# Sample scores of the far cache rows: from transposes and products on TensorE to row sums on VectorE

## The chip, the core and the metric

The kernel runs on one core of a Trainium2 chip. The metric is device time in microseconds from the start to the end of one execution. A core has a matrix engine (PE; its weight loads are listed apart as PEld), VectorE (DVE), ScalarE (ACT), GpSimd (POOL), and SyncE (SP), which in this kernel issues nearly all the DMA transfers. Every engine works through its own instructions in order.

## The reference

One decoder layer works on a prompt of 2048 positions and on a sample: 8 batch rows of 8 new positions each, which follow a cache of 2048 older keys and values per batch row.

```python
h = _rmsnorm(x, norm_g)
z = jnp.einsum('bsd,dc->bsc', h, w_in)          # u, va, ga, q, k, vb, gb, each 512 wide
...
def _dilated_branch_sample(q, k_all, v_all, dil, n_strides):
    idx = w_buf + jnp.arange(T)[:, None] - dil * jnp.arange(n_strides + 1)[None, :]
    kg = k_all[:, idx]
    vg = v_all[:, idx]
    s = jnp.einsum('bthe,btjhe->bthj', q, kg).astype(jnp.float32) * (E ** -0.5)
    p = jnp.exp(s - m)
    o = jnp.einsum('bthj,btjhe->bthe', p, vg.astype(jnp.float32)) / den[..., None]
```

The sample attends with (window, dilation) = (128, 1), (512, 4) and (2048, 16), 8 heads of 64. So for a cache row further back than 512, new position t needs it only if its distance is a multiple of 16: of the first 1536 cache rows, t sees those whose index is t modulo 16, 96 of them. The last 512 rows are seen by several positions under masks. The prompt attends to itself with the same three dilations; gates, norms and an output projection follow.

## The kernel before, in words

The work is done in three stages, all laid out by one Python function whose order a scheduler then turns into one list per engine.

Stage 1 projects q, k and v of the prompt, tile after tile of 128 positions. A projection is a chain of 24 matrix products on two-part float16 operands (`product`, L258 to L275; the instruction is on L265), each 128x128 weights against 512 columns. I call these the dense products. Stage 2 is the prompt's attention, with mixer A's products between. Stage 3 (class `Fin`) does gate products (`ps_p`), merges the branches, and multiplies by `w_out` (`ps_y`), again 24 dense products to a chain.

The sample attention runs between the dense products of stage 1 (batch rows 0 to 4) and of stage 3 (batch rows 5 to 7; `NB1 = 5`). A generator, `Sample.batches`, hands out one small step at a time. After each dense product `pull_sample` credits it 216 ns times a rate (0.9 and 0.8), and a step costs `STEP1` or `STEP3`, so the two constants set how thickly the steps lie among the dense products. The small products are float32.

For one batch row the cache is read in `NC = 5` chunks of 128 partitions x 2 rows x 512 (`kr`, 512 KB, a ring of 3 buffers, loaded two chunks ahead by SP, L490). Chunks 0 to 3 are rows 16p+2g and 16p+2g+1, so they hold residues 0 to 7 of all 2048 rows; chunk 4 has the other residues of the last 512. Each chunk takes:

- 8 transposes on PE into PSUM (`ps_k`, L595), and two copies by ACT to SBUF (`kt`, L598);
- 8 products with the batch row's queries (`ps_q`, L499; 12 in the last chunk, which adds the new keys), 16 columns each: two heads by 8 positions. Every row is scored against all 8 positions, and a mask that VectorE adds (L507) throws most of that away.

`attend` then takes the maximum over all rows (VectorE L516; PE `ps_x` L520), subtracts it (PE `ps_b` L527, VectorE L528), exponentiates (ACT L529), sums (VectorE L530, PE `ps_n` L535), and multiplies the cached values in chunks `vr` (`ps_o`, L548: 8 products of 16 columns a chunk, 44 in all, after one product with zeros, L539). The score tile `sm` has `NK = 11` columns of 64.

Of the kernel before, what the change touches and what calls it, by code (L numbers as in the profile page):

```python
# [83 lines left out]
STEP1 = 250.0  # L84
STEP3 = 333.0
NK = 11
# [26 lines left out]
def kernel_body(tc, a):  # L113
# [34 lines left out]
    vsd = dram.tile([64, W], F32, name="vsd")  # L148
    hd = dram.tile([S + 64, W], F32, name="hd")
# [178 lines left out]
    def row_scale(t, x):  # L328

        n = P if t < NT else 64  # L330
        sq = [ph1.tile([P, 4, P], F32, name="sq", tag="sq") for _ in range(2)]
        for s_, x_ in zip(sq, x):
            small["sq", t] = act.activation(s_[:, :, :n], x_, AF.Square).ins
        a_, b_ = (s_[:, :, :n] for s_ in sq)
        pool.tensor_tensor(a_, a_, b_, op=ALU.add)
        dve.tensor_add(b_[:, 0:2], a_[:, 0:2], a_[:, 2:4])
        dve.tensor_add(b_[:, 0], b_[:, 0], b_[:, 1])
        ps = psR.tile([P, W], F32, name="ps_r", tag="R")
        small["r", t] = pe.matmul(ps[:n, 0:1], b_[:, 0], ones[:, 0:1], start=True, stop=True).ins
# [12 lines left out]
        return rb  # L352
# [71 lines left out]
    def operand(pool_, i, load=False):  # L424

        o = ops[i] = pool_.tile([P, DB, 4, 2 * T] if i == 0 else [P, 4, P], F32, name=("qbd", "ktn")[i], bufs=1)
# [43 lines left out]
    class Sample:  # L470
# [5 lines left out]

        def __init__(self, sam, samk, pso, step):
            self.sam, self.samk, self.step = sam, samk, step
            self.mask = const(samk, "smask", [P, 10 + DB, T], a["c_smask"])
            self.ps = pso.tile([P, W], F32, name="ps_q", bufs=1)  # L480
            self.po = pso.tile([P, 4, 2 * T], F32, name="ps_o", bufs=1)
            self.raws = {"kr": {}, "vr": {}}

        def load(self, c, key, u):
# [5 lines left out]
            sp.dma_start(r.rearrange("p n c -> p (n c)"), cache_rows(c, *u))  # L490

        def scores(self, b, g, kts, sm):

            o = (g // 2 % 2) * 4 + (g % 2) * 2
            for i in range(2 if g < NC - 1 else 3):
                for j in range(4):
                    c = (o + i) * G + j * 2 * T
                    k = kts[j // 2][:, j % 2, i * P:(i + 1) * P] if i < 2 else ops[1][:, j]
                    ii = pe.matmul(self.ps[:, c:c + 2 * T], k, ops[0][:, b, j], start=True, stop=True)  # L499
                    yield  # L500
            done.append(ii.ins)
            if g in (0, 2):
                return
            o = (g // 2 % 2) * 4
            lo = 4 * (g // 2)
            for i, n, m in ((0, 4, lo),) if g < NC - 1 else ((0, 2, lo), (2, 1, 10 + b)):
                dve.tensor_tensor(sm[:, lo + i:lo + i + n].rearrange("p n (c t) -> p n c t", t=T),  # L507
                                  self.ps[:, (o + i) * G:(o + i + n) * G].rearrange("p (n c t) -> p n c t", n=n, t=T),
                                  self.mask[:, m:m + n, None, :].to_broadcast([P, n, 8, T]), op=ALU.add)

        def attend(self, b, sm):
# [27 lines left out]
            keep(pe.matmul(po.rearrange("p j c -> p (j c)"), self.raws["vr"][(b, 0)][:, 0, 0:P], zero,  # L539
                           start=True, stop=False), "v")  # L540
            for g in range(NC):
# [25 lines left out]
        def batches(self, bs, keys_done=None):  # L567
# [8 lines left out]
            chunks = [(b, g) for b in bs for g in range(NC)]  # L576
# [5 lines left out]
            for b, g in chunks + [(None, g) for g in range(NC)]:  # L582
                if b is not None:
                    if g == 0:
                        sms[b] = self.sam.tile([P, NK, G], F32, name="sm", tag="sm", bufs=3)
                    kr = self.raws["kr"].pop((b, g))
                    self.load(ck, "kr", next(nxt, None))
                kts = []
                for x in range(2):
                    if b is not None:  # L590
# [6 lines left out]
                        kt = self.samk.tile([P, 2, 2 * P], F32, name="kt", tag="ktt", bufs=4)  # L597
                        act.activation(kt, ps, AF.Copy)  # L598
                        kts.append(kt)
                    if x and late:  # L600
# [3 lines left out]
                        if u[1] == NC - 1:  # L604
# [5 lines left out]
                if b is not None:  # L610
# [44 lines left out]
    def direct(t, raws, behind_=()):  # L655
# [3 lines left out]
        for g in range(0 if xg else 2):  # L659
            x = samk.tile([P, 4, P], F32, name="xg", tag="ktt", bufs=4)  # L660
# [708 lines left out]
def _constants():  # L1369
# [30 lines left out]
    p, i = np.arange(P), np.arange(10)[:, None]  # L1400
    key = np.where(i < 8, 16 * p + i, PAST - 4 * P + 16 * (p // 4) + 2 * (p % 4) + i).ravel()
# [4 lines left out]
    m = np.where(n > 0, 8.0 * np.log(np.maximum(n, 1)), NEG).reshape(10 + DB, P, T).transpose(1, 0, 2)  # L1406
# [45 lines left out]
```

## Time and profile before

| | us |
|---|---|
| median of 3 runs | 1211.02 |
| lowest, highest | 1210.85, 1211.27 |
| the profiled execution's own time | 1207.28 |
| its span, first to last instruction | 1205.5 |
| PE busy | 1146.0 (95%) |
| VectorE busy | 786.8 (65%) |
| ScalarE busy | 619.8 (51%) |
| granted PE clock, mean | 0.973 |

The span is what the profile sees; 1.8 us lie around it, and the profiled execution is 3.7 us under the median. A product's row has a duration that overlaps the next one, so what a product costs PE is the time from its start to the next start. A float32 product with 16 columns leaves two rows (two passes), a transpose one.

### The profile page before, as it was taken

The page shows a single profiled execution, that of the slowest core. Times are in us where ns is not written, and L with a number is a line of the kernel's source. Part 1 is how long each engine was busy: PE and PEld are TensorE (multiplying, and loading weights), DVE is VectorE, ACT ScalarE, POOL GpSimd, SP SyncE. Part 2 cuts the span into 40 slices and gives each one's busy share as a digit, 9 for nine tenths or more (in the row PEclk, how much of TensorE's full clock was granted, in tenths as well). Part 3 has the DMA queues.
Part 4 walks back from the last instruction along what each step waited for, and adds up shares of the span by engine and source line. Part 5 has one row for each costly group of instructions (what it writes and reads, how often), then busy time and mean ns, then how long its engine had stood idle before and what let it go on. Part 6 is the DMA issues. An engine that isn't in the chain of part 4 may idle for free. (4 is left out here: it accounts for less than half of the span.)

```text
span 1205.5 us, 23117 instructions
## 1 busy us (share of the span) xinstructions
PE 1146.0 (95%) x8402; PEld 752.3 (62%) x8402; DVE 786.8 (65%) x2332; ACT 619.8 (51%) x1341; POOL 274.9 (23%) x296
## 2 busy tenths in 40 slices
PE   7799999999999889999999999899989999999997
PEld 2347787877767346665766676566636667676543
DVE  7864445444442677877887887878955565665874
ACT  5564434343442746666776777867843332322332
POOL 4432122112110033243334334432300000000110
PEclk9899999999997999999999999999989999999999
DMA  8687676767572997879979978997699868576753
GB/s 272 203 299 221 186 222 198 241 194 214 172 232 81 246 228 170 142 137 228 180 145 194 222 132 180 194 177 126 155 322 335 236 202 235 162 189 184 208 137 96
DMA packets 299026, 237.98 MB, mean 197 GB/s; under 512 B 189920, under 2 KB 240096, under 8 KB 298912
## 3 DMA queue, kind: packets, MB, share of 16 engines
q1 hardware_dynamic: 272848, 210.58, 70.3%
q10 hardware_dynamic: 26064, 25.92, 7.4%
q8 instruction: 66, 1.08, 0.4%
q14 instruction: 48, 0.39, 0.1%
HBM read 128.38 MB, written 63.24 MB: 159 GB/s over the span
## 5 line engine op out<-in xcount | busy, mean ns | idle before, releaser
L265 PEld LDWEIGHTS <-xh 128*128 128x128 f16 x2712 | 288.7, 113 | 218.4 <-issue 30.2
L945 DVE CUSTOM_DVE_ANT_0 sm<-ps_s,mk,qsi 128x256 f32<-128x256 f32 (+1 forms) x384 | 145.1, 420 | 59.0 <-PE ps_s L940 44.0
L953 ACT ACTIVATE sm<-sm,st 128x256 f32<-128x256 f32 (+1 forms) x384 | 145.6, 450 | 57.6 <-DVE st L948 52.2
L265 PE MATMUL ps_y<-wh_o,cT 128*128 128x512 f16 x528 | 169.1, 380 | 0.0
L975 POOL TENSOR_TENSOR p<-sm,p 128x256 f16<-128x256 f32 (+1 forms) x128 | 112.8, 887 | 228.5 <-ACT p L974 202.9
L153 POOL TENSOR_TENSOR sc<-sc,powers 128x1 f32<-128x1 f32 (+3 forms) x51 | 31.5, 618 | 410.6 <-DVE sc L1151 189.4
L499 PEld LDWEIGHTS ps_q<-qbd,kt 128*128 128x128 f32 x640 | 107.9, 189 | 24.2 <-DVE sm L507 1.9
L548 PEld LDWEIGHTS ps_o<-sm,vr 128*128 128x128 f32 x640 | 109.2, 201 | 22.0 <-issue 1.1
L265 PEld LDWEIGHTS <-cT 128*128 128x128 f16 x800 | 82.0, 114 | 55.4
L265 PE MATMUL ps_y<-wl_o,cT 128*128 128x512 f16 x272 | 103.4, 380 | 0.0
L991 PE MATMUL ps_o<-vt,pT 128*128 128x65 f16 x600 | 78.9, 194 | 16.4 <-DMA pT<-p 16.2
L548 PE MATMUL ps_o<-sm,vr 128*128 128x16 f32 x640 | 93.5, 239 | 0.0
L499 PE MATMUL ps_q<-qbd,kt 128*128 128x16 f32 x640 | 91.1, 224 | 1.4 <-DVE sm L507 1.4
L265 PE MATMUL ps_p<-wh_v,xh 128*128 128x512 f16 x264 | 88.2, 382 | 2.1 <-DVE z L281 2.1
L265 PE MATMUL ps_p<-wh_va,xh 128*128 128x512 f16 x264 | 85.0, 389 | 3.4 <-ACT vt L384 3.0
L265 PE MATMUL ps_p<-wh_k,xh 128*128 128x512 f16 x248 | 82.5, 385 | 5.7 <-DVE xh L254 4.1
L265 PE MATMUL ps_p<-wh_gb,xh 128*128 128x512 f16 x264 | 86.7, 385 | 1.0 <-DVE u L1080 1.0
L265 PE MATMUL ps_p<-wh_u,xh 128*128 128x512 f16 x264 | 83.9, 379 | 1.7 <-DVE z L281 1.7
L265 PE MATMUL ps_p<-wh_ga,xh 128*128 128x512 f16 x264 | 85.4, 385 | 0.0
L936 PE MATMUL ps_s<-k,q 128*128 128x256 f16 (+1 forms) x384 | 83.0, 257 | 0.0
L940 PE MATMUL ps_s<-k,q 128*128 128x256 f16 (+1 forms) x384 | 82.2, 255 | 0.0
L598 ACT ACTIVATE kt<-ps_k 128x512 f32<-128x512 f32 x80 | 46.8, 591 | 65.0 <-PE ps_k L595 64.6
(308 smaller groups left out, 2578.8 us busy)
## 6 DMA issues: line engine op xcount, KB each, us to landing
vr<-cache_v SPq DMA_DIRECT2D x40, 512.0 KB
kr<-cache_k SPq DMA_DIRECT2D x40, 512.0 KB
xh<-xd SPq DMA_DIRECT2D x32, 512.0 KB
raw<-w_in SPq DMA_DIRECT2D x52, 256.0 KB
brd<-ob ACTq DMA_DIRECT2D x48, 264.0 KB
bt<-brd SPq DMA_DIRECT2D x16, 792.0 KB
vt<-vd ACTq DMA_DIRECT2D x48, 258.0 KB
vd<-vs SPq DMA_DIRECT2D x32, 258.0 KB
```

Source lines behind the costliest of these rows:

```text
L153: pool.tensor_tensor(out, src, powers[:out.shape[0], 0, 0:n], op=ALU.pow)
L265: ii = pe.matmul(out, l, r[:, k], start=(k == 0 and i == 0), stop=(k == 7 and i == len(ops) - 1))
L499: ii = pe.matmul(self.ps[:, c:c + 2 * T], k, ops[0][:, b, j], start=True, stop=True)
L548: ii = pe.matmul(po[:, j], v, sm[:, 2 * g + i, j * 2 * T:(j + 1) * 2 * T], start=False, stop=(g == NC - 1 and i == 2 and j == 3))
L598: act.activation(kt, ps, AF.Copy)
L936: ii = pe.matmul(out, q, kv[0], start=True, stop=False)
L940: keep(pe.matmul(out, q, kv[1], start=False, stop=True), "s")
L945: dve.tensor_tensor_reduce(sm[:, y].rearrange("p b k -> p (b k)")[:, 0:n], out, m, qsi[:, 3:4], -3e38, op0=ALU.add, op1=ALU.max, accum_out ...
L953: act.activation(sv, sv, AF.Exp, bias=self.st[:, 4 + u:5 + u], scale=1.0)
L975: (pool, dve)[x in DVELO].tensor_tensor(lo, sv, hi, op=ALU.subtract)
L991: keep(pe.matmul(po[:, u, 0:E + 1], hi, vv[:, vi, j, 0:E + 1], start=(b == 0), stop=False), "o")
```

## The change

Cache rows over 512 back are no longer scored on PE. The chunks become six, worked through in the order `KORD`: four far chunks of 96 partitions (`FAR`), where partition p holds rows 16p+2g and 16p+2g+1 of the first 1536, and two near chunks with the last 512 rows (four adjacent rows to a partition). The near chunks are transposed and scored as before. In a far chunk each of the two rows of a partition belongs to one new position t; its query row, kept in DRAM (`qsd`), is loaded broadcast to 96 partitions (`qb`, 192 KB), and VectorE multiplies the key row by it in place and sums each head's 64 elements (`far`). One column of `sm` then holds all far scores, with no mask, and the tile has 6 columns of 64 rather than 11. In `attend` a far value product has 96 rows of weights and 2 columns. `qb` shares the ring of `kt`, now 7 or 8 buffers rather than 4. `STEP1` and `STEP3` go up.

```diff
-STEP1 = 250.0
-STEP3 = 333.0
-NK = 11
+STEP1 = 310.0
+STEP3 = 480.0
+NK = 6
+FAR = 96
...
-        dg = ph1.tile([P, P], F32, name="dg", tag="dg")
+        dg = ph1.tile([P, P], F32, name="dg", tag="dg", bufs=1)
...
                 sample_operands(qk, i)
+                if i == 0:
+                    sp.dma_start(qsd, qk)
...
-            sp.dma_start(flat, opd[i])
+            sp.dma_start(flat, opd[i][:, b0 * 8 * T:] if i == 0 else opd[i])
...
-    NC = 5
+    NC = 6
+    FSTEP = 2
+    KORD = (0, 1, 4, 2, 3, 5)
...
         if g < 4:
-            return c[b].rearrange("(p r) c -> p (r c)", r=16)[:, 2 * g * W:(2 * g + 2) * W]
-        first = c[b, PAST - 4 * P + 8:PAST - 4 * P + 9, 0:1]
-        return bass.AP(tensor=c.tensor, offset=first.offset, ap=[[16 * W, 32], [2 * W, 4], [1, 2 * W]])
+            return c[b, 0:FAR * 16].rearrange("(p r) c -> p (r c)", r=16)[:, 2 * g * W:(2 * g + 2) * W]
+        return c[b, FAR * 16:].rearrange("(p r) c -> p (r c)", r=4)[:, 2 * (g - 4) * W:(2 * g - 6) * W]
...
+            self.kts = 7 if sam is samk else 8
...
-            sp.dma_start(r.rearrange("p n c -> p (n c)"), cache_rows(c, *u))
+            b, g = u
+            n = FAR if g < 4 else P
+            sp.dma_start(r[0:n].rearrange("p n c -> p (n c)"), cache_rows(c, b, g))
+            if key == "kr" and g < 4:
+                qs = self.qbs[u] = []
+                for t in (2 * g, 2 * g + 1):
+                    qs.append(self.samk.tile([P, W], F32, name="qb", tag="ktt", bufs=self.kts))
+                    sp.dma_start(qs[-1][0:FAR], qsd[b * T + t:b * T + t + 1].to_broadcast([FAR, W]))
...
+        def far(self, g, kr, qb, sm):
+
+            yield
+            for i in range(2):
+                k = kr[0:FAR, i]
+                ii = dve.tensor_tensor(k, k, qb[i][0:FAR], op=ALU.mult)
+                tc.add_manual_dep(ii.ins, tc_prod[0].name, AFTER, reason="not ahead of its place among the products")
+                o = sm[0:FAR, 0].rearrange("p (h t) -> p t h", t=T)[:, 2 * g + i]
+                dve.tensor_reduce(o, k.rearrange("p (h e) -> p h e", e=E), axis=AX.X, op=ALU.add)
+            yield
...
-                        v = (vr[:, i] if i < 2 else self.vn)[:, j * P:(j + 1) * P]
-                        ii = pe.matmul(po[:, j], v, sm[:, 2 * g + i, j * 2 * T:(j + 1) * 2 * T],
-                                       start=False, stop=(g == NC - 1 and i == 2 and j == 3))
+                        c = slice(j * 2 * T, (j + 1) * 2 * T)
+                        if g < 4:
+                            t = slice(2 * g + i, None, T)
+                            ii = pe.matmul(po[:, j, t], vr[0:FAR, i, j * P:(j + 1) * P], sm[0:FAR, 0, c][:, t],
+                                           start=False, stop=False)
...
                     if g == 0:
                         sms[b] = self.sam.tile([P, NK, G], F32, name="sm", tag="sm", bufs=3)
+                        dve.memset(sms[b][FAR:, 0], NEG)
...
                 for x in range(2):
-                    if b is not None:
+                    if far:
+                        next(fw)
+                        for _ in range(FSTEP):
+                            yield self.step
+                    elif b is not None:
...
-            x = samk.tile([P, 4, P], F32, name="xg", tag="ktt", bufs=4)
+            x = samk.tile([P, 4, P], F32, name="xg", tag="ktt", bufs=8)
```

PE, in the middle of stage 1, before: transposes of a key chunk (`ps_k`), each behind a dense product (`ps_p`).

```order
L595 MATMUL ps_k<-ident,kr 128x128
L265 LDWEIGHTS xh
L265 MATMUL ps_p<-wh_k,xh 128x512
L595 MATMUL ps_k<-ident,kr 128x128
L265 LDWEIGHTS xh
L265 MATMUL ps_p<-wh_k,xh 128x512
L595 MATMUL ps_k<-ident,kr 128x128
L265 LDWEIGHTS xh
L265 MATMUL ps_p<-wl_k,xh 128x512
L595 MATMUL ps_k<-ident,kr 128x128
```

And now, in the middle of stage 1, where values of a far chunk are multiplied (`ps_o`, 2 columns) and a far chunk of keys leaves no row on PE.

```order
L574 MATMUL ps_o<-sm,vr 128x2
L267 LDWEIGHTS xh
L267 MATMUL ps_p<-wh_k,xh 128x512
L574 MATMUL ps_o<-sm,vr 128x2
L267 LDWEIGHTS xh
L267 MATMUL ps_p<-wh_k,xh 128x512
L267 LDWEIGHTS xh
L267 MATMUL ps_p<-wl_k,xh 128x512
L267 LDWEIGHTS xh
L267 MATMUL ps_p<-wh_k,xh 128x512
```

Of 40 transposes and 44 score products a batch row, 16 and 20 are left; the value products become 52 (32 far, 20 near), and more dense products stand next to each other.

VectorE in stage 1, now: the products and sums of a far chunk (`kr`, `sm`) stand between the steps of the prompt's tiles (`vs`, `ss`, `dg`, `sq`) and of `attend` (`mx`).

```order
L545 TENSOR_REDUCE mx<-ps_x 64x1
L546 TENSOR_SCALAR mx<-ident,mx 64x64
L417 MEMSET vs 128x8
L418 SCALAR_TENSOR_TENSOR vs<-vt,qsc,vs 128x8x64
L529 TENSOR_TENSOR kr<-kr,qb 96x512 x2
L343 TENSOR_SCALAR ss<-ps_r 128x1
L532 TENSOR_REDUCE sm<-kr 96x8 x2
L338 TENSOR_TENSOR sq<-sq 128x256
L349 TENSOR_SCALAR dg<-ident,ss 128x128
L339 TENSOR_TENSOR sq<-sq 128x128
L552 TENSOR_TENSOR sm<-sm,ps_b 128x384
L554 TENSOR_REDUCE mx<-sm 128x64
```

Four such rows a far chunk, 16 a batch row, are new; a far chunk whose `kr` or `qb` has not landed holds up the rows behind it.

PE at the end of stage 1, before: the values of batch row 4 (`ps_o`) with few dense products left.

```order
L548 MATMUL ps_o<-sm,vr 128x16 x2
L535 MATMUL ps_n<-mx,ones 128x64
L548 MATMUL ps_o<-sm,vr 128x16 x22
...
L548 MATMUL ps_o<-sm,vr 128x16 x16
L548 MATMUL ps_o<-sm,vn 128x16
```

The same place now; where rows are left out stand 5 dense products before, and 6 now.

```order
L574 MATMUL ps_o<-sm,vr 128x2 x2
L559 MATMUL ps_n<-mx,ones 128x64
L574 MATMUL ps_o<-sm,vr 128x2 x22
...
L574 MATMUL ps_o<-sm,vr 128x2 x8
```

The first run keeps its length, and the second goes from 17 products to 8.

## Rows read from the trace of the kernel before

**Rows 1.** The page, part 1: busy time, share of the span and instructions by engine.

```profile
PE 1146.0 (95%) x8402; PEld 752.3 (62%) x8402; DVE 786.8 (65%) x2332; ACT 619.8 (51%) x1341; POOL 274.9 (23%) x296
```

**Rows 2.** Busy us by stretch: length, PE, PEld, DVE, ACT, POOL; clock, DMA share, GB/s.

```profile
40.00:50.00 10.00, 5.07 (x15) 1.89 (x14) 9.88 (x20) 5.87 (x12) 5.43 (x4) 0.91 0.32 98
...
103.00:350.00 247.00, 246.61 (x1766) 191.60 (x1767) 111.44 (x246) 102.79 (x165) 46.29 (x43) 1.00 0.68 208
...
365.00:383.00 18.00, 18.00 (x80) 14.98 (x80) 1.99 (x7) 2.02 (x4) 0.00 (x0) 0.53 0.29 86
...
890.00:905.00 15.00, 11.48 (x45) 5.54 (x43) 12.86 (x36) 8.41 (x16) 0.42 (x1) 0.77 1.06 387
905.00:1125.00 220.00, 220.00 (x1421) 151.55 (x1420) 131.26 (x265) 65.99 (x138) 12.92 (x21) 0.99 0.77 218
```

**Rows 3.** Timeline of PE in stage 1: start us, us, what, count.

```profile
304.07 0.29 PE L499 MATMUL ps_q<-qbd,kt 128*128 128x16 f32 x2
304.21 0.38 PE L265 MATMUL ps_p<-wh_k,xh 128*128 128x512 f16 x1
304.43 0.29 PE L499 MATMUL ps_q<-qbd,kt 128*128 128x16 f32 x2
...
304.78 0.60 PE L595 MATMUL ps_k<-ident,kr 128*128 128x128 f32 x4
305.22 0.29 PE L499 MATMUL ps_q<-qbd,kt 128*128 128x16 f32 x2
```

**Rows 4.** Timeline of PE in stage 1, at the value products.

```profile
340.88 0.29 PE L548 MATMUL ps_o<-sm,vr 128*128 128x16 f32 x2
341.02 0.38 PE L265 MATMUL ps_p<-wl_q,xh 128*128 128x512 f16 x1
```

**Rows 5.** Instructions of a line: count, duration ns least/median/most, first and last start.

```profile
L595 PE MATMUL ps_k<-ident,kr x320: 270/273/447, 76.0 to 1056.5; 128*128 128x128 f32 x160
L499 PE MATMUL ps_q<-qbd,kt x640: 176/262/283, 88.1 to 1075.1; 128*128 128x16 f32 x160
```

**Rows 6.** The same view, of VectorE's lines.

```profile
L1304 DVE TENSOR_TENSOR bt<-bt x16: 674/682/695, 897.4 to 1168.6; 128x512 f32<-128x512 f32 x16
...
L1299 DVE TENSOR_REDUCE mm<-dd x16: 158/180/183, 893.0 to 1164.4; 128x8 f32<-128x24 f32 x16
...
L521 DVE TENSOR_REDUCE mx<-ps_x x8: 272/282/283, 128.4 to 1090.7; 64x1 f32<-64x128 f32 x8
...
L516 DVE TENSOR_REDUCE mx<-sm x8: 1352/1362/1381, 121.6 to 1079.2; 128x64 f32<-128x704 f32 x8
```

**Rows 7.** Timeline around a product with 64 rows of weights (`ps_b`).

```profile
307.55 0.38 PE L265 MATMUL ps_p<-wh_v,xh 128*128 128x512 f16 x1
...
307.86 0.29 PEld L527 LDWEIGHTS ps_b<-mx,ones 64*128 64x128 f32 x2 [0.42 <-issue]
307.86 0.43 PE L527 MATMUL ps_b<-mx,ones 64*128 64x64 f32 x2
...
308.22 0.39 PE L265 MATMUL ps_p<-wh_v,xh 128*128 128x512 f16 x1
```

**Rows 8.** Timeline of PE at the end of stage 1.

```profile
362.65 6.80 PE L548 MATMUL ps_o<-sm,vr 128*128 128x16 f32 x44
369.29 0.59 PE L265 MATMUL ps_p<-wh_q,xh 128*128 128x512 f16 x1
```

**Rows 9.** Timeline of PE where the sample's part of stage 3 begins.

```profile
895.24 0.38 PE L265 MATMUL ps_p<-wh_gb,xh 128*128 128x512 f16 x1
899.13 1.94 PE L595 MATMUL ps_k<-ident,kr 128*128 128x128 f32 x8 [3.52 <-issue]
```

**Rows 10.** What SP's queue waited for: us in total, times, longest.

```profile
SPq L490 <- PE ps_o L548: 67.5, 25, 7.4
...
SPq L490 <- PE ps_k L595: 29.0, 19, 4.8
```

**Rows 11.** The page, part 2: DMA packets and bytes of the span.

```profile
DMA packets 299026, 237.98 MB, mean 197 GB/s; under 512 B 189920, under 2 KB 240096, under 8 KB 298912
```

More of the change, by code (lines that the diff above doesn't have):

```diff
@@ L148, in kernel_body @@
     vsd = dram.tile([64, W], F32, name="vsd")
+    qsd = dram.tile([64, W], F32, name="qsd")
     hd = dram.tile([S + 64, W], F32, name="hd")
@@ L424, in operand @@
     def operand(pool_, i, load=False):
-        o = ops[i] = pool_.tile([P, DB, 4, 2 * T] if i == 0 else [P, 4, P], F32, name=("qbd", "ktn")[i], bufs=1)
+        b0 = NB1 if load else 0
+        o = ops[i] = pool_.tile([P, DB - b0, 4, 2 * T] if i == 0 else [P, 4, P], F32, name=("qbd", "ktn")[i], bufs=1)
         flat = o.rearrange("p b j t -> p (b j t)") if i == 0 else o.rearrange("p j k -> p (j k)")
         if load:
-            sp.dma_start(flat, opd[i])
+            sp.dma_start(flat, opd[i][:, b0 * 8 * T:] if i == 0 else opd[i])
         else:
@@ L478, in __init__ @@
             self.sam, self.samk, self.step = sam, samk, step
-            self.mask = const(samk, "smask", [P, 10 + DB, T], a["c_smask"])
+            self.b0 = NB1 if sam is samk else 0
+            self.kts = 7 if sam is samk else 8
+            self.mask = const(samk, "smask", [P, 4 + DB, T], a["c_smask"])
             self.ps = pso.tile([P, W], F32, name="ps_q", bufs=1)
             self.po = pso.tile([P, 4, 2 * T], F32, name="ps_o", bufs=1)
-            self.raws = {"kr": {}, "vr": {}}
+            self.raws, self.qbs = {"kr": {}, "vr": {}}, {}
         def load(self, c, key, u):
@@ L489, in load @@
             r = self.raws[key][u] = pool_.tile([P, 2, W], F32, name=key, tag=key, bufs=3)
-            sp.dma_start(r.rearrange("p n c -> p (n c)"), cache_rows(c, *u))
+            b, g = u
[6 more added lines that the diff above has]
+                    sp.dma_start(qs[-1][0:FAR], qsd[b * T + t:b * T + t + 1].to_broadcast([FAR, W]))
         def scores(self, b, g, kts, sm):
-            o = (g // 2 % 2) * 4 + (g % 2) * 2
-            for i in range(2 if g < NC - 1 else 3):
+            x = g - 4
+            o = 4 * x
+            for i in range(2 + x):
                 for j in range(4):
@@ L498, in scores @@
                     k = kts[j // 2][:, j % 2, i * P:(i + 1) * P] if i < 2 else ops[1][:, j]
-                    ii = pe.matmul(self.ps[:, c:c + 2 * T], k, ops[0][:, b, j], start=True, stop=True)
+                    ii = pe.matmul(self.ps[:, c:c + 2 * T], k, ops[0][:, b - self.b0, j], start=True, stop=True)
                     yield
             done.append(ii.ins)
[L502 to L507, printed above, removed]
+            for i, n, m in ((0, 2, 2 * x), (2, 1, 4 + b))[:1 + x]:
+                dve.tensor_tensor(sm[:, 1 + 2 * x + i:1 + 2 * x + i + n].rearrange("p n (c t) -> p n c t", t=T),
                                   self.ps[:, (o + i) * G:(o + i + n) * G].rearrange("p (n c t) -> p n c t", n=n, t=T),
                                   self.mask[:, m:m + n, None, :].to_broadcast([P, n, 8, T]), op=ALU.add)
+        def far(self, g, kr, qb, sm):
[7 more added lines that the diff above has]
+            yield
         def attend(self, b, sm):
@@ L538, in attend @@
             zero = ops[1][:, 0, DB * T:]
-            keep(pe.matmul(po.rearrange("p j c -> p (j c)"), self.raws["vr"][(b, 0)][:, 0, 0:P], zero,
+            keep(pe.matmul(po.rearrange("p j c -> p (j c)"), self.raws["vr"][(b, 0)][0:FAR, 0, 0:P], zero[0:FAR],
                            start=True, stop=False), "v")
@@ L546, in attend @@
                     for j in range(4):
-                        v = (vr[:, i] if i < 2 else self.vn)[:, j * P:(j + 1) * P]
-                        ii = pe.matmul(po[:, j], v, sm[:, 2 * g + i, j * 2 * T:(j + 1) * 2 * T],
-                                       start=False, stop=(g == NC - 1 and i == 2 and j == 3))
+                        c = slice(j * 2 * T, (j + 1) * 2 * T)
[3 more added lines that the diff above has]
+                                           start=False, stop=False)
+                        else:
+                            v = (vr[:, i] if i < 2 else self.vn)[:, j * P:(j + 1) * P]
+                            ii = pe.matmul(po[:, j], v, sm[:, 2 * g - 7 + i, c],
+                                           start=False, stop=(g == NC - 1 and i == 2 and j == 3))
                         keep(ii, "v")
@@ L575, in batches @@
             bs = list(bs)
-            chunks = [(b, g) for b in bs for g in range(NC)]
+            chunks = [(b, g) for b in bs for g in KORD]
             nxt = iter(chunks)
@@ L588, in batches @@
                 kts = []
+                far = b is not None and g < 4
+                if far:
+                    fw = self.far(g, kr, self.qbs.pop((b, g)), sms[b])
                 for x in range(2):
-                    if b is not None:
+                    if far:
+                        next(fw)
+                        for _ in range(FSTEP):
+                            yield self.step
+                    elif b is not None:
                         ps = psT.tile([P, 2, 2 * P], F32, name="ps_k", tag="T")
@@ L596, in batches @@
                                 yield self.step
-                        kt = self.samk.tile([P, 2, 2 * P], F32, name="kt", tag="ktt", bufs=4)
+                        kt = self.samk.tile([P, 2, 2 * P], F32, name="kt", tag="ktt", bufs=self.kts)
                         act.activation(kt, ps, AF.Copy)
@@ L603, in batches @@
                             yield self.step
-                        if u[1] == NC - 1:
+                        if u[1] == KORD[-1]:
                             self.active.append(self.attend(u[0], sms.pop(u[0])))
@@ L609, in batches @@
                         yield from self.stage(work)
-                if b is not None:
+                if b is not None and not far:
                     late.append((b, g, kts, sms[b]))
@@ L1399, in _constants @@
     t = np.arange(T)
-    p, i = np.arange(P), np.arange(10)[:, None]
-    key = np.where(i < 8, 16 * p + i, PAST - 4 * P + 16 * (p // 4) + 2 * (p % 4) + i).ravel()
+    p, i = np.arange(P), np.arange(4)[:, None]
+    key = (PAST - 4 * P + 4 * p + i).ravel()
     own = np.where(p // T == np.arange(DB)[:, None], PAST + p % T, 10 * PAST).ravel()
@@ L1405, in _constants @@
     n = sum(((dist >= 0) & (dist <= P * d) & (dist % d == 0)).astype(int) for d in (1, 4, 16))
-    m = np.where(n > 0, 8.0 * np.log(np.maximum(n, 1)), NEG).reshape(10 + DB, P, T).transpose(1, 0, 2)
+    m = np.where(n > 0, 8.0 * np.log(np.maximum(n, 1)), NEG).reshape(4 + DB, P, T).transpose(1, 0, 2)
     out["c_smask"] = np.ascontiguousarray(m.astype(f))
```

## The prediction

> **What bounds the kernel now.** I read the page's busy times first, then the table by stretch, then PE's timeline, then what PE and SP wait for.
>
> By the busy times PE is at 95% and no other engine is over 65% [rows 1]. The table by stretch says where [rows 2]: in the two stretches that hold the sample attention, 103 to 350 us and 905 to 1125 us, PE is busy 246.61 of 247.00 us and 220.00 of 220.00. It never waits there. VectorE is busy 45% and 60% of these stretches, ScalarE 42% and 30%, the DMA engines 68% and 77%. So there the time is the sum of what PE has to do, and each product taken off its list shortens the kernel by its own start-to-start time, as long as nothing else becomes late.
>
> That time is read from the timeline [rows 3, 4]. A dense product takes 304.43 - 304.21 = 0.22 us. A score product takes 304.21 - 304.07 = 0.14 us, although it streams 16 columns. Four transposes take 305.22 - 304.78 = 0.44 us, 0.11 each. A value product takes 341.02 - 340.88 = 0.14 us.
>
> **The change part by part.**
>
> *PE's list.* Counts by batch row, 8 of them: transposes 40 to 16, scores 44 to 20, values 44 to 52. (The trace has 320 transposes [rows 5], which is 8 x 40.) So 192 transposes go, 192 x 0.11 = 21.1 us; 192 scores go, 192 x 0.14 = 26.9 us; 64 values come, 64 x 0.14 = 9.0 us. Net 39.0 us less, five eighths of it (24.4) in stage 1 and three eighths (14.6) in stage 3. All of it lies on the path, since PE does not wait in either place.
>
> The far value products are a new kind: 96 rows of weights, 2 columns. The trace has no such row. From below, their price is that of a transpose, 0.11 us: a product of 16 columns already costs 0.14, so its columns are not what it pays for. From above, there is a product with 64 rows of weights, `ps_b` [rows 7]. It starts 307.86 - 307.55 = 0.31 us after a dense product that needs 0.22, because its weights are not loaded until the product before is done (PEld stands idle 0.42 us and begins at 307.86 too), and the dense product behind it starts 0.36 us later, 0.45 in all. On 256 far value products that is 0.31 us more each, 79 us. I take 0.14, nearest in shape and type: the same matrix, three quarters of its rows.
>
> On this the Trainium skill has a rule, "TensorEngine Tiling (Array Packing)", sections Tiling Modes and Key Properties: a change of tiling mode drains the engine, and modes exist for 128, 64 and 32 rows. Rows 7 agree with the drain for 64 rows. By the page 96 rows fit no mode but the one of 128, there is no drain, and the sum stays at 39 us less; without that rule rows 7 could be stretched to 96 rows, and the sum would be 40 us more. No row here shows 96.
>
> *The clock at the end of stage 1.* Batch row 4's values come when the dense products run out: 22 in a row take 6.80 us [rows 8], and from 365 to 383 us the granted clock is 0.53, that is mostly 1.2 instead of 2.4 GHz, while PE is busy throughout [rows 2]. The 18 us lose about 8.5. The order now has the same first run, but the second has 8 products instead of 17. Nine at 6.80/22 = 0.31 us are 2.8 us less of the slow stretch. As they cost 0.17 more than the 0.14 already counted, and the dense products behind them get the full clock sooner, I take 2 us of gain (bounds 0 and 5).
>
> *VectorE.* A far chunk adds two products of 96x512 and two sums of 512 to 8, a batch row 8 of each. The product is bounded closely by a row of the same length, 0.68 us [rows 6]. For the sum the nearest rows are 24 elements to 8, 0.18 us, and 128 to 1, 0.28 us: 0.98 ns an element, so 0.18 + 488 x 0.98 ns = 0.66 us. From above, the sum over 704 strided elements takes 1.36, which for 512 would be 0.99. I take 0.66; the elements of a head lie next to each other. That is 8 x 1.34 = 10.7 us a batch row, up to 13.4. The two reductions over the score tile shrink from 704 elements to 384, 1.36 to about 0.74, 1.2 us less; net 9.5 us. Stage 1 gets 47 us more and stage 3 28. VectorE's load over the two stretches becomes about (111 + 40)/225 = 67% and (131 + 28)/206 = 77%. It stays under PE, which is what hides this. If that cover went, it would cost what VectorE is late by, at most these 75 us.
>
> *Waits that are new.* A far product waits on VectorE for three transfers (`kr` and two `qb`), and behind it stand the steps that the prompt's tiles need. Before, PE waited for `kr` itself, and it did so once, 3.52 us, at the beginning of stage 3 [rows 9], where the DMA engines are full (1.06) [rows 2]. SP now waits for VectorE before it may overwrite `kr`, where it waited 29.0 us in 19 times for the transposes [rows 10], and the loads and stores behind it on SP wait along; PE did not notice that in 905 to 1125. I bound what PE loses by 0 and by 3.52 us in every batch row, 28 us. I take 5, near the lower end, since a chunk is asked for two chunks ahead and PE has only these 3.52 us in the trace to show for all 40 key loads.
>
> *DMA.* Keys and values are the same bytes as before (4 x 384 + 2 x 512 KB against 5 x 512). The 64 broadcast loads add 64 x 96 x 2 KB = 12.6 MB to 238 [rows 11], 5%, in stretches with shares of 0.68 and 0.77 [rows 2]. Hidden. Eight of them and the store of `qsd` fall into the beginning, where the share drops to 0.32 between 40 and 50 us [rows 2]; I take nothing, with 2 us to either side.
>
> *The rest.* One `dg` buffer instead of two, the larger `xg` ring, the shorter operand load, a memset of 32 partitions a batch row, 48 fewer copies on ScalarE: each is off PE's list and hidden by PE's work; nothing.
>
> *Sum.* 1207.3 - 39.0 - 2 + 5 = 1171.3 for the profiled execution. The median of the runs stands 3.7 above that execution, so 1175.
>
> **The rivals.**
>
> *The far value products drain PE.* Place: the 256 products with 96 rows. Price 0.31 us each as from rows 7, 79 us, so 1175 + 79 = 1254. It decides from a price of 0.30 us a product on (0.14 + 40/256). For it: the only row with fewer than 128 rows of weights shows it. Against: 96 rows are more than half of the array, the far side of what that row has. This is the one that ends slower. The Trainium skill's page named above has no mode of 96 rows and speaks against it too.
>
> *VectorE or its transfers are late.* Waits as in rows 9 in every batch row: 23 us over the 5 that I took, 1198. For it: a chunk now lasts only a few dense products when `attend` has nothing to do, VectorE has up to 77% to do in order, and dense products of stage 3 need VectorE to empty their PSUM buffers. Against: rows 2, PE gapless with SP waiting a great deal.
>
> *More than the list.* The new waits do not come, and the beginning of stage 3 runs on: the 3.52 us gap of rows 9 goes, as PE's first rows there no longer need the first `kr`, and with it the low clock of 890 to 905 (0.77, some 3.4 us). 1175 - 5 - 3.5 - 3.4 = 1163.
>
> *It does not pay.* The steps are priced higher and spread wider, and what PE saves returns as waiting in order for products whose inputs are late. 1211. Against: the dense products need nothing from the sample.
>
> **How the numbers follow.** My forecast holds 0.62 (1166 to 1187), the list and more 0.13 (1157 to 1166), late VectorE 0.13 (1187 to 1205), the drain 0.09, no gain 0.03. The range leaves out the drain, no gain, and the tips of the others: 1160 to 1201. A measurement of this kernel can tell 0.2%, 2.4 us, from no change. Faster 0.62 + 0.13 + 0.13 = 0.88, same 0.02, slower 0.10 (the drain and a little of no gain).
>
> **What would show it.** PE's rows must be 192 transposes and 192 scores fewer, still gapless in the sample's stretches, with dense products 0.22 us apart. A far value product between two dense ones must take 0.14 us; 0.4 and an idle PEld before it is the drain. VectorE's new rows must take 0.68 and 0.66 us. The forecast is wrong if PE shows idle time before `ps_q`, `ps_x` or a dense product with VectorE or a DMA as the releaser, summing to more than 10 us, or if the granted clock drops in new places, where float32 products now run without dense ones between.

## The result, and the profile after

The changed kernel takes 1203.5 us in the median of 16 runs (1191.8 to 1214.5); the kernel before, beside it, 1211.6 (1208.4 to 1217.2). The ratio, which compares means, is 0.991, 95% interval 0.988 to 0.993. So the kernel is faster by 8 us in the medians and 11 by the ratio, where 36 were forecast, and its time is above the forecast's range (1160 to 1201). Two of the 16 runs, the slowest, are left out of the ratio and of the means below. The profiled execution took 1203.4 us, with a span of 1201.6.

The page's busy times, to be read against [rows 1]:

```profile
PE 1125.5 (94%) x7954; PEld 703.1 (59%) x7954; DVE 841.9 (70%) x2460; ACT 592.2 (49%) x1293; POOL 279.1 (23%) x296
```

The table by stretch of the changed kernel, same columns as [rows 2]:

```profile
103.00:350.00 247.00, 236.87 (x1516) 165.43 (x1515) 142.11 (x314) 88.40 (x141) 48.81 (x43) 0.96 0.81 235
365.00:383.00 18.00, 18.00 (x89) 14.16 (x89) 1.60 (x5) 1.41 (x2) 0.00 (x0) 0.62 0.32 104
890.00:905.00 15.00, 9.15 (x32) 3.89 (x32) 13.78 (x28) 5.67 (x12) 0.64 (x1) 0.77 1.05 244
905.00:1125.00 220.00, 212.67 (x1207) 127.20 (x1208) 153.79 (x320) 57.62 (x128) 16.13 (x23) 0.97 0.94 244
```

This is the result in four lines. PE, gapless before, now stands idle 247 - 236.87 = 10.1 us in the first long stretch and 7.3 in the last, and the granted clock is 0.96 and 0.97 where it was 1.00 and 0.99. The transfers take 0.81 and 0.94 of the DMA engines' time instead of 0.68 and 0.77. Over the whole span PE is idle 1201.6 - 1125.5 = 76.1 us, where it was 1205.5 - 1146.0 = 59.5.

What PE waited for in 40 to 368 us, in total, times and longest; first the two largest of before, then the changed kernel:

```profile
PE ps_p L265 <- DVE xh L254: 4.1, 1, 4.1
PE ps_p L265 <- DVE z L281: 2.1, 1, 2.1
```

```profile
PE ps_p L267 <- ACT qk L374: 5.0, 3, 3.3
PE ps_k L633 <- DMA kr<-cache_k: 4.6, 1, 4.6
PE ps_p L267 <- DVE xh L256: 3.9, 1, 3.9
PE ps_b L551 <- DVE mx L546: 2.2, 1, 2.2
PE ps_k L633 <- ACT kt L636: 1.5, 1, 1.5
```

The new waits have many releasers: cache rows, ScalarE's copy of a dense product (`qk`), a maximum on VectorE. Ahead of ScalarE there is a transfer again. What its squares (`sq`) waited for in the same stretch, before and after:

```profile
ACT sq L333 <- DMA xt<-xT: 35.7, 13, 5.4
```

```profile
ACT sq L335 <- DMA xt<-xT: 61.6, 14, 10.6
```

ScalarE works in order. While it stands at the squares of a tile that has not landed, the copies that empty PE's buffers stand behind it.

One gap in PE's timeline of the changed kernel (start, us, what, count, idle before):

```profile
97.13 0.59 PE L267 MATMUL ps_p<-wh_v,xh 128*128 128x512 f16 x2
102.36 1.09 PE L633 MATMUL ps_k<-ident,kr 128*128 128x128 f32 x4 [4.64 <-DMA kr<-cache_k]
103.24 0.63 PE L267 MATMUL ps_p<-wl_v,xh 128*128 128x512 f16 x1
103.67 0.42 PE L633 MATMUL ps_k<-ident,kr 128*128 128x128 f32 x1
```

and the stretch it lies in, as in the table above:

```profile
100.20:107.00 6.80, 4.64 (x15) 2.83 (x16) 5.09 (x13) 2.13 (x4) 0.00 (x0) 0.50 0.88 252
```

Behind the gap of 4.64 us a dense product takes 103.67 - 103.24 = 0.43 us, twice its usual time: the granted clock is 0.50, so 1.2 GHz, until 107. This gap is paid twice. At the same time VectorE stood 6.00 us at a far product:

```profile
94.04 0.74 DVE L404 SCALAR_TENSOR_TENSOR q<-qk,qsc,q 128x512 f16<-128x512 f32 x1
100.78 1.29 DVE L529 TENSOR_TENSOR kr<-kr,qb 96x512 f32<-96x512 f32 x2 [6.00 <-DMA kr<-cache_k]
```

**Two sums instead of one.** Each run has a span and a mean granted clock. Span times (1 - clock) is the time lost to the low clock; the rest is about what the kernel would take at 2.4 GHz throughout. The loss is an upper figure, since low clock counts in it while PE stands idle too. Single runs of one kernel scatter by 1 to 4 us (standard deviation) in the rest. Times and ratios first, then means over the runs compared:

| kernel | median us | ratio to before, 95% | lost to clock | rest |
|---|---|---|---|---|
| before (six times) | 1209.7 to 1212.8 | 1 | 32.0 to 34.7 | 1176.0 to 1177.2 |
| changed | 1203.5 | 0.991 (0.988 to 0.993) | 40.1 | 1159.1 |
| e1, one query row | 1187.1 | 0.978 (0.975 to 0.981) | 35.6 | 1149.1 |
| e2, no far sums | 1204.7 | 0.992 (0.990 to 0.995) | 43.5 | 1158.5 |
| e3, resident sums | 1205.4 | 0.995 (0.992 to 0.998) | 46.1 | 1158.3 |
| e4, even steps | 1192.7 | 0.985 (0.980 to 0.989) | 44.1 | 1148.4 |
| e5, small loads | 1189.9 | 0.982 (0.978 to 0.986) | 39.4 | 1148.4 |
| e6, paired loads | 1202.7 | 0.994 (0.991 to 0.996) | 44.7 | 1156.9 |
| e7, even, paired | 1192.1 | 0.985 (0.982 to 0.988) | 40.9 | 1150.6 |
| e8, even, one query row | 1177.8 | 0.974 (0.970 to 0.977) | 38.3 | 1138.7 |
| e9, before, 40 more loads | 1227.0 | 1.011 (1.008 to 1.014) | 37.3 | 1186.1 |
| e10, even, shuffled | 1179.1 | 0.973 (0.971 to 0.976) | 35.1 | 1142.5 |
| e11, wider, shuffled | 1195.4 | 0.986 (0.983 to 0.988) | 47.7 | 1145.3 |
| e12, widest steps | 1204.8 | 0.994 (0.991 to 0.996) | 47.7 | 1155.1 |
| e13, close, shuffled | 1192.5 | 0.986 (0.983 to 0.988) | 42.4 | 1148.7 |
| e14, wider, sooner | 1193.1 | 0.986 (0.983 to 0.990) | 40.1 | 1151.0 |
| e15, shuffled, sooner | 1195.0 | 0.987 (0.985 to 0.990) | 44.6 | 1148.3 |
| e16, before, 64 copies | 1211.6 | 1.000 (0.997 to 1.003) | 29.4 | 1180.4 |
| e17, copies for loads | 1204.3 | 0.994 (0.992 to 0.997) | 47.1 | 1155.5 |

### The profile page after: what moved, and what is told of

It is laid out like the page before. It is cut to its first block, busy times and chain, and to the rows that moved or that the text cites. A ratio compares the mean times of both kernels' runs of the same rounds, so it can differ in the third digit from the quotient of the medians.

```text
span 1201.6 us, 22400 instructions
## 1 busy us (share of the span) xinstructions
PE 1125.5 (94%) x7954; PEld 703.1 (59%) x7954; DVE 841.9 (70%) x2460; ACT 592.2 (49%) x1293; POOL 279.1 (23%) x296
## 3 DMA queue, kind: packets, MB, share of 16 engines
q1 hardware_dynamic: 280352, 223.09, 75.9%
## 5 line engine op out<-in xcount | busy, mean ns | idle before, releaser
L267 PEld LDWEIGHTS <-xh 128*128 128x128 f16 x2712 | 278.8, 111 | 243.6 <-issue 38.4
L574 PEld LDWEIGHTS ps_o<-sm,vr 96*128 96x128 f32 x512 | 90.9, 204 | 25.3 <-issue 2.6
L1029 PE MATMUL ps_o<-vt,pT 128*128 128x65 f16 x600 | 78.3, 193 | 11.7 <-DMA pT<-p 11.7
L267 PE MATMUL ps_p<-wh_q,xh 128*128 128x512 f16 x224 | 78.7, 396 | 4.2 <-ACT qk L374 4.2
L1030 PE MATMUL ps_o<-vt,pT 128*128 128x64 f16 x600 | 78.3, 195 | 0.0
L1031 PE MATMUL ps_o<-vt,pT 128*128 128x65 f16 x600 | 77.2, 193 | 0.0
L574 PE MATMUL ps_o<-sm,vr 96*128 96x2 f32 x512 | 73.1, 228 | 1.4 <-ACT sm L553 1.4
```

The lines of the kernel that those rows point to most:

```text
L267: ii = pe.matmul(out, l, r[:, k], start=(k == 0 and i == 0), stop=(k == 7 and i == len(ops) - 1))
L574: ii = pe.matmul(po[:, j, t], vr[0:FAR, i, j * P:(j + 1) * P], sm[0:FAR, 0, c][:, t], start=False, stop=False)
L1029: keep(pe.matmul(po[:, u, 0:E + 1], hi, vv[:, vi, j, 0:E + 1], start=(b == 0), stop=False), "o")
L1030: keep(pe.matmul(po[:, u, 0:E], hi, vv[:, vi, j, E + 1:VW], start=False, stop=False), "o")
L1031: keep(pe.matmul(po[:, u, 0:E + 1], lo, vv[:, vi, j, 0:E + 1], start=False, stop=last), "o")
```

## The experiments

**VectorE's share.** e2 leaves its far work out, e3 lets it wait for nothing.

```diff
 e2, in far()
-  dve.tensor_tensor(k, k, qb[i][0:FAR], op=ALU.mult)
-  dve.tensor_reduce(o, k.rearrange(...), axis=AX.X, op=ALU.add)
 e3, in far()
-  k = kr[0:FAR, i]
+  k = self.one[0:FAR]              # resident, all ones
-  dve.tensor_tensor(k, k, qb[i][0:FAR], op=ALU.mult)
+  dve.tensor_tensor(k, k, k, op=ALU.mult)
```

> Leaves out the 64 far products and 64 far row sums on VectorE; the far scores are set to a constant; the transfers of cache rows and query rows stand, and nothing reads them. Theory 'late rows': VectorE no longer stands at a far product for its rows, but transposes still wait for theirs: 1180-1192. Theory 'busy VectorE': 1175-1185, and the next kernel (sums on a resident tile) stays at 1203. Theory 'bytes': nothing changes in the traffic, 1200-1205.

> All 128 VectorE instructions stand, with the same sizes, but they multiply and sum a resident tile of ones in place of the cache rows and query rows, so they wait for no transfer (far scores are not the reference's); all transfers stand. Theory 'late rows': as good as leaving them out, within 3 us of that kernel (1180-1192). Theory 'busy VectorE': 1200-1205 as the changed kernel. Theory 'bytes': 1200-1205.

Neither moved anything: 0.992 and 0.995, the rest within 1 us of the changed kernel's. Without VectorE's 128 instructions (0.71 and 0.67 us each, below) PE waits elsewhere. Its largest wait of e2 in 40 to 368 us:

```profile
PE ps_p L267 <- ACT qk L374: 11.7, 5, 5.7
```

So "busy VectorE" falls, and so does "late rows" as far as it went by VectorE.

**The query loads.** e1 takes their bytes and their number away, e5 gives back the number alone, e6 halves the number.

```diff
 e1, in load()
-  for t in (2 * g, 2 * g + 1):
-      qs.append(self.samk.tile([P, W], F32, name="qb", ...))
-      sp.dma_start(qs[-1][0:FAR], qsd[...].to_broadcast([FAR, W]))
+  if not self.qres: ...            # one tile, loaded once a stage
+  self.qbs[u] = self.qres * 2
 e5, as e1, and
+  sp.dma_start(q1[0:1], qsd[b * T + t:b * T + t + 1])
 e6
+  q2 = self.samk.tile([P, 2, W], F32, name="qb", tag="qb", bufs=2)
+  sp.dma_start(q2[0:FAR]..., qsd[r0:r0 + 2]...to_broadcast([FAR, 2 * W]))
```

> Leaves out the 64 loads of query rows (12.6 MB): each stage loads one query row once and every far product multiplies by that one tile, so the scores of the far rows are not the reference's; all other transfers and all instructions stand. If the added bytes and issues are what the changed kernel loses (theory 'bytes'), it comes to 1175-1185 us against 1203.5. If the cost is that short far chunks ask for their cache rows too late (theory 'late rows'), only a part comes back: 1192-1199, with VectorE still waiting for kr. If VectorE's own time is the cost (theory 'busy VectorE'): 1201-1205.

> Separates the bytes of the query loads from their number. As the kernel with one resident query row (1187 us), but the 64 loads are issued again at their places, each of one row on one partition (2 KB in place of 192 KB), into the same ring of buffers, and nothing reads them. Theory 'bytes' (12.6 MB more on the 16 DMA engines make every transfer beside them late): 1185-1190. Rival 'issues' (each issue occupies SP's queue and each transfer its fixed time, whatever its size): 1198-1205, as the changed kernel.

> Exact result. Each far chunk's two query rows come in one transfer of 384 KB (4 KB on each partition) instead of two of 192 KB: 32 issues for 64, half the packets, the same bytes, in a ring of its own of two; the ring of transposed tiles goes back to 4 buffers (3 in the last stage). Theory 'bytes': 1198-1205. Rival 'issues' (or packets): 1190-1196, half of the 16 us come back.

e1 is 0.978, and its 1187.1 us lie between what "bytes" and "late rows" had set: 10.0 us of the rest come back and 4.5 of the clock. The page's busy times and the table by stretch of e1, and its wait of `sq`:

```profile
PE 1104.9 (94%) x7954; PEld 692.0 (59%) x7954; DVE 837.4 (71%) x2460; ACT 593.3 (50%) x1293; POOL 275.5 (23%) x296
103.00:350.00 247.00, 246.81 (x1614) 173.30 (x1615) 145.66 (x320) 97.75 (x161) 47.85 (x43) 0.99 0.77 225
905.00:1125.00 220.00, 218.25 (x1291) 134.26 (x1290) 162.88 (x341) 62.49 (x142) 16.38 (x26) 0.99 0.87 227
```

```profile
ACT sq L335 <- DMA xt<-xT: 36.2, 16, 3.7
```

PE is gapless again in the first stretch, and ScalarE's wait is back at 36 us. But over its span of 1179.6 us this execution leaves PE idle 74.7 us, hardly less than the changed kernel's 76.1. It is the fastest run of e1, and what it gained is clock (0.979, where the changed kernel's profile has 0.962). So the 10 us of the rest stand on the means of the runs, not on this trace.

e5, with 64 issues of 2 KB, has the same rest (1148.4): it is the bytes, not the issues. Pairing them (e6) gains nothing to speak of (1156.9). e1 also takes `qb` out of the ring that it shares with `kt`; so does e6, so the ring is not the cause.

ScalarE's wait at `xt` is no measure of the loss. In e5, and in e8 below, which has the lowest rest of all, it is:

```profile
ACT sq L335 <- DMA xt<-xT: 51.3, 17, 8.0
```

```profile
ACT sq L335 <- DMA xt<-xT: 47.0, 16, 7.0
```

By which waits the bytes come to PE in the changed kernel is therefore not shown.

Each version is scheduled anew, and the order of the lists shifts with it: 332 of the 7954 places in PE's list hold another product in e1 than in the changed kernel. No run holds the order fixed. Against order as the cause of the 10 us speaks that the rest is 1156.9 to 1159.1 in the four closely spaced kernels with these bytes (changed, e2, e3, e6) and 1148.4 to 1149.1 in the three without (e1, e5, and e13 below).

**The converse.** The kernel before gets such traffic too: e9 by 40 loads into two buffers, e16 by 64 copies that wait for no buffer. e17 puts the same copies into e1.

```diff
 e9, on the kernel before, beside each kr of a residue, stage 1
+  q = self.samk.tile([P, W], F32, name="dq", tag="dq", bufs=2)
+  sp.dma_start(q[0:96], c[u[0], t:t + 1].to_broadcast([96, W]))
 e16, on the kernel before, both stages; e17, on e1, from qsd
+  self.dq = dram.tile([96, W], F32, name=...)
+  sp.dma_start(self.dq, ....to_broadcast([96, W]))
```

> The converse, on the kernel before: its stage 1 gets 40 transfers more, two beside each load of cache rows of residues, 192 KB each (one row of the cache to 96 partitions, 7.9 MB), into a ring of two buffers; nothing reads them, every other instruction stands (one small tile, dg, has one buffer for two, for room). Theory 'bytes' (traffic makes transfers late for any kernel): TensorE's list is as long as before but the time rises by 8-18 us, 1220-1230, with ScalarE's wait for xt longer. Rival 'only because TensorE's list is shorter' (before has cover for late transfers): within 4 us of before, 1208-1216.

> The converse without a ring to wait for. The kernel before gets 64 transfers more, two beside each load of cache rows of residues, each of 192 KB (one cache row, 96 times), into memory of their own off the core, so none waits for a buffer; nothing reads them, every other instruction stands. Theory 'bytes': 8-14 us more than before, 1219-1226, most of it time at full clock. If the loss of the kernel with 40 loads into two buffers came from SP's queue standing at those buffers (30.1 us in its trace): within 4 us of before, 1207-1216.

> The changed kernel with one resident query row (1187.1 us; the far scores are not the reference's), and in place of each of the 64 query loads a copy of the same 192 KB into memory off the core, at the same place, waiting for no buffer. The converse on the kernel before cost it no time; so either the changed kernel, with its shorter list, has no cover for such traffic, or only loads into the core's own memory cost. 'Any traffic': 1196-1204, near the 1203.5 with the loads. 'Only the loads': 1185-1190. The copies took the DMA engines some 28 us of all sixteen's time in the kernel before, the loads some 48 in the changed one, so a middle (1192-1197) speaks for engine time by its amount.

e9 was slower by 13 us, in the range of "bytes", but it mixes two things. SP's queue, then ScalarE, then PE, from its trace:

```profile
148.51 9.29 SPq L494 DMA_DIRECT2D dq<-cache_k  x5
157.90 0.37 SPq L229 DMA_DIRECT2D xt<-xT  x1
```

```profile
161.70 0.63 ACT L333 ACTIVATE sq<-xt 128x512 f32<-128x512 f32 x1 [15.43 <-DMA xt<-xT]
162.24 0.58 ACT L602 ACTIVATE kt<-ps_k 128x512 f32<-128x512 f32 x1
```

```profile
162.87 0.90 PE L599 MATMUL ps_k<-ident,kr 128*128 128x128 f32 x3 [11.40 <-ACT kt L602]
```

Five added loads keep SP 9.29 us, `xt` is issued behind them, ScalarE stands 15.43 us at its squares, the copy of the transposed keys stands behind that, and PE 11.40 us for that copy. It shows how a late load comes to PE, not that bytes did it. e16, without the two buffers, is at 1.000 (its rest is 4 us more, its clock loss 4 to 5 less). e17 is at 0.994, against e1's 0.978: 17 us by the medians, 6.4 of them in the rest and 11.5 in the clock, although the copies go to other memory. But the copies did not stay beside the loads that they were placed with. They wait for no buffer, and all 64 were issued in the first 141 us, while the loads of the changed kernel are spread over 1013. Count, duration in ns, first and last start, of e16, e17 and the changed kernel:

```profile
L494 SPq DMA_DIRECT2D dq<-cache_k x64: 490/545/1734, 25.7 to 136.6; - x64
L509 SPq DMA_DIRECT2D dq<-qsd x64: 469/532/2182, 29.1 to 140.9; - x64
L506 SPq DMA_DIRECT2D qb<-qsd x64: 303/420/7052, 29.7 to 1012.8; - x64
```

(The added loads of e9 were all issued by 158 us, too.) So the pair shows what a burst of these bytes at the beginning costs: nothing under the longer list, 17 us under the shorter one. That bytes spread out as the real loads are would be covered under the longer list it does not show; none of them fall in 905 to 1125 us. The first long stretch of e16 and then e17, and what `sq` waited for in 40 to 368 us:

```profile
103.00:350.00 247.00, 242.71 (x1713) 185.91 (x1712) 105.61 (x236) 97.55 (x160) 46.27 (x43) 0.99 0.78 233
103.00:350.00 247.00, 238.68 (x1463) 167.09 (x1462) 140.81 (x301) 84.74 (x136) 47.51 (x43) 0.93 0.81 240
```

```profile
ACT sq L333 <- DMA xt<-xT: 50.0, 14, 7.2
ACT sq L335 <- DMA xt<-xT: 60.1, 19, 11.4
```

ScalarE waits longer for `xt` in both, 50.0 us for 35.7 and 60.1 for 36.2, but only the kernel with the shorter list loses time. The Trainium skill says ("DMA: Bandwidth & Descriptors", Issuing engines are not separate DMA queues) that all transfers end on the same 16 engines and interleave there, whoever issues them. No run here tests that, since SP issues the copies as it issues `xt`.

**The spacing.** Far chunks had 4 places among the dense products, then 16 (e4), with the query loads paired (e7), or with one query row (e8); then 32 (e12).

```diff
 e4 (e7 = with e6's loads, e8 = with e1's)     e12
-FSTEP = 2; STEP1 = 310.0; STEP3 = 480.0
+FSTEP = 8; STEP1 = 219.0; STEP3 = 340.0      # 16; 158.0; 244.0
```

> The same work, but a far chunk takes 16 places among the dense products instead of 4 (FSTEP 8 for 2) and the step costs are scaled so that the sample work ends where it did (219 for 310, 340 for 480). Far chunks then last as long as chunks with transposes, so that two chunks ahead is more time. Theory 'late rows': 1180-1192, the waits of VectorE and TensorE for kr gone. Theories 'bytes' and 'busy VectorE': 1200-1205.

> Exact result. Paired query loads with the even spacing of the far chunks (FSTEP 8, step costs 219 and 340; 1192.7 us without the pairing). Theory 'bytes' (what counts is how many bytes are asked for in a short time): 1190-1194, the pairing adds nothing. Rival 'issues': 1182-1188.

> Even spacing, and one resident query row in place of the 64 loads (the far scores are not the reference's). It asks whether spacing and bytes are one cause or two. If spacing helps only because it spreads the query loads' bytes ('one cause'): 1184-1188, as with one query row alone (1187.1). If chunks that are too short cost something of their own ('two causes'): 1174-1181, the 25 and 19 us nearly add, and the forecast's 1175 is met.

> Exact result. The changed kernel with its query loads, and far chunks of 32 places (FSTEP 16, step costs 158 and 244), so that a far chunk's 768 KB have about as much time per byte as the 512 KB of a chunk with transposes. If what counts is bytes asked for in a short time: 1184-1190, better than FSTEP 8 (1192.7). If only their sum counts: 1190-1196.

e4 takes 10.7 us off the rest, and in its 40 to 368 us neither PE nor VectorE waits for `kr`. That this is why is not shown: PE's wait for `kr` in the changed kernel was 4.6 us there, and without VectorE's waits (e2) nothing was gained. e8 takes 10.4 off e1's rest: spacing and bytes are two causes that add. Its rest is 1138.7, 38 us under before: the list's 39 us are there to be had. e7 is like e4; pairing is nothing. But e12 missed: with 32 places most is lost again (1155.1 and 47.7).

**A version with fewer bytes.** A query row is loaded to partitions 0, 32 and 64 only, and VectorE spreads it.

```diff
 e10, on e4
-  sp.dma_start(qs[-1][0:FAR], qsd[...].to_broadcast([FAR, W]))
+  sp.dma_start(q[0:FAR:32], qsd[...].to_broadcast([FAR // 32, W]))
 ...
+  dve.stream_shuffle(qb[i][0:FAR], qb[i][0:FAR], [0] * 32)
 e11  FSTEP 12, STEP1 183, STEP3 284     e13  FSTEP 2, 310, 480
 e14  FSTEP 12, STEP1 168, STEP3 284     e15  FSTEP 8, 206, 340
```

> Exact result. Even spacing (FSTEP 8), and each query row is loaded to 3 partitions (0, 32, 64: 6 KB in place of 192 KB) and spread to the 96 by a stream_shuffle of VectorE ahead of the product: 12.2 MB fewer, 64 VectorE instructions of some 0.6 us more (an estimate from the product of the same 96x512: 0.65 us). Theory 'bytes': as with one resident query row and even spacing, 1177-1184, since leaving out VectorE's 128 instructions moved nothing. Rival 'VectorE has no room for 64 more' : 1186-1195.

> Exact result. As the kernel with shuffled query rows, with far chunks of 24 places (FSTEP 12, step costs 183 and 284) in place of 16. If the distance between loads still counts when the query bytes are gone: 1172-1178. If it is already enough: within 3 us of that kernel.

> Exact result. Only the bytes are taken from the changed kernel: shuffled query rows (6 KB a row), spacing and step costs as changed (FSTEP 2, 310, 480). If bytes and spacing are two causes: 1186-1192, as with one resident query row (1187). If spacing alone makes the shuffled kernel's 1179 (the bytes then add nothing, as the two wider kernels could suggest): 1198-1204.

> Exact result. Shuffled query rows with far chunks of 24 places (1195.4 us at step cost 183 in the first stage), its step cost 168, so that the sample work of that stage ends some 75 dense products earlier. The trace of the 1195.4 us kernel showed 24 us at half clock around the last sample products (361 to 385 us). If the place of that end (few dense products left to put between) is why it is slower: 1178-1185. If the wider far chunk itself is slower: 1192-1198.

> Exact result. The shuffled kernel of 1179.1 us (FSTEP 8) with step cost 206 for 219 in the first stage, so that the sample work ends some 55 dense products earlier. If the half-clock stretches at the end of the first stage (352.9 to 366.6 us) are owed to that end: 1172-1178. If the sample products as such bring them, wherever they stand: 1178-1183.

e10 leaves nothing out and takes 1179.1 us, 0.973 (0.971 to 0.976): faster than both kernels. VectorE's far work in it (line numbers have moved):

```profile
L535 DVE TENSOR_TENSOR kr<-kr,qb 96x512 f32<-96x512 f32 x64 | 47.2, 763 | 0.1
L533 DVE STREAM_SHUFFLE qb<-qb 96x512 f32<-96x512 f32 x64 | 43.5, 726 | 0.0
L537 DVE TENSOR_REDUCE sm<-kr 96x8 f32<-96x512 f32 x64 | 41.9, 677 | 0.0
```

43.5 us more on VectorE for 12.2 MB less cost at most the 3.8 us by which e10's rest is over e8's. e13 has the bytes' gain without the spacing (rest 1148.7, as e1). The other three gained nothing: wider, or ending sooner, none came under 1193. e11 and e15 missed both of their ranges; e14 came out in the range for "the wider far chunk itself is slower". In e15 only a step cost of stage 1 differs from e10's, by 6%, and it is 16 us slower: 5.8 in the rest and 9.5 in the clock. The end of the sample work in the profiled runs of e10 and e15, the clock third from the end:

```profile
350.00:378.00 28.00, 28.00 (x164) 20.50 (x164) 9.05 (x30) 12.08 (x27) 0.00 (x0) 0.82 0.47 134
```

```profile
350.00:378.00 28.00, 28.00 (x135) 23.46 (x135) 2.85 (x9) 7.57 (x19) 0.00 (x0) 0.57 0.46 141
```

PE is busy throughout in both; one has 0.82 of the clock there, the other 0.57. The two kernels have the same products in another order, and the stretch holds more of them in e10 (164 rows, 135 in e15). What makes the difference in clock stays open. e14, whose sample work ends sooner than e11's, got 7.6 us of clock back and lost 5.7 in the rest, so the place of the end is at most a part of it. Why e12 and e11 are slower than 16 places is open, too.

## Why the prediction was wrong

*PE's list (39.0 us): right.* The rest of e8 is 38 us under before. Its page shows the list without that split: PE is busy 1106.2 us, 39.8 less than before, at nearly the same clock (0.972, before 0.973):

```profile
PE 1106.2 (94%) x7954; PEld 695.9 (59%) x7954; DVE 841.3 (72%) x2460; ACT 591.8 (50%) x1293; POOL 275.4 (23%) x296
```

The far value product, the new kind that I bounded by 0.11 and 0.45, came at my 0.14:

```profile
140.17 0.28 PE L574 MATMUL ps_o<-sm,vr 96*128 96x2 f32 x2
140.32 0.38 PE L267 MATMUL ps_p<-wh_q,xh 128*128 128x512 f16 x1
```

The next dense product starts 0.15 us later, with no drain as in [rows 7]. What I had concluded from the Trainium skill's list of modes ("TensorEngine Tiling (Array Packing)", Tiling Modes), no drain for 96 rows, agrees with these rows.

*VectorE (0.68 and 0.66 us an instruction, hidden): right.* The rows of the changed kernel:

```profile
L529 DVE TENSOR_TENSOR kr<-kr,qb 96x512 f32<-96x512 f32 x64 | 43.2, 713 | 16.0 <-DMA kr<-cache_k 14.8 <-DMA qb<-qsd 1.2
L532 DVE TENSOR_REDUCE sm<-kr 96x8 f32<-96x512 f32 x64 | 41.2, 673 | 0.0
```

They are 0.71 and 0.67, and e2 shows that nothing is gained without them.

*Waits that are new (5 us): this is the step that failed.* The rest fell by 17.4 us in place of 39, so the waits are 21.6 us where I took 5: 10 by the bytes of the query loads (e1, e5, e13), 10 by the close spacing of the far chunks (e4, e8). e17 gives 6.4 in the rest for the same bytes in a burst. The 21.6 are within my bounds of 0 and 28, but I took the lower end for a wrong reason: that PE had only one such wait to show. That one I also misread: [rows 9] puts the 3.52 us down to "issue", nothing that the profile shows, and not to `kr`. PE was gapless in the trace because its own list was the longest; that said nothing on how late transfers would be for a shorter one. ScalarE's 35.7 us at `xt` were in the trace of before, and I had not read them.

*DMA (hidden): wrong in the changed kernel.* For the list of before, e16 cost no time, with the copies in a burst. I held 5% of bytes against shares of 0.68 and 0.77. But the 5% are of the whole span, and 45 of the 64 loads were issued in the two stretches, 467 us of it: there the traffic rose from 208 to 235 GB/s and from 218 to 244, 13% and 12%, and the shares to 0.81 and 0.94.

*The clock (2 us of gain): wrong sign.* The loss rose from about 33.5 to 40.1 us. At the end of stage 1 the clock did rise, from 0.53 to 0.62, as I had it, but low stretches came elsewhere, as at 100.2 to 107 us behind a gap. I counted waits at their length; that one was followed by dense products at half speed.

The sum is then 1211 - 39 + 21.6 + 6.6 = 1200. It closes by construction, as the last two terms are taken from the measured runs. The rival "VectorE or its transfers are late" had the right half in its second word: the transfers. VectorE's own part is nothing that e2 or e3 shows, and the loss is larger than the rival's price (1198).

## What to carry to other kernels

A gapless engine hides how late everything else is. Before work is taken off it, read what the other engines wait for and how full the DMA engines are in that stretch, and set added bytes against the traffic of that stretch, not of the whole span. A burst of bytes that cost nothing under the longer list cost 17 us under the shorter one. Split a measured difference into time lost to the clock and the rest, since a wait on TensorE can be paid a second time in clock, and since a 6% change of pacing (e10, e15) moved the clock's part by 9.5 us with the work unchanged. When a copy or load is added as a control, look where it was issued.

## What had not been expected of the hardware

A `stream_shuffle` of 96x512 in place takes 0.73 us, about a product of that size, and replaces 192 KB of transfer by 6. The share of the DMA engines did not price the added transfers: the 64 copies brought queue 1 from 70.3% to 72.8% of the span in e16, some 28 us of all sixteen engines, and from e1's 73.2% to 76.3% in e17, some 58; the loads brought it from e1's 73.2% to 75.9%, some 48. A stretch of sample products with PE busy throughout ran at 0.57 of the clock in e15 and at 0.82 in e10, with the same products in another order.
